# Head tiles staged in two pairs of spare rows, three half projections among the output projections, row stores on the ACT queue, second-product blocks of three pairs

## The chip, the cores and the metric

The kernel runs on one core of a Trainium2 chip, in one launch. The metric is the device time of a run in microseconds (us); lower is better. The engines that matter here are PE (TensorE, the matmuls), DVE (VectorE), ACT (ScalarE), POOL (GpSimd) and SP (SyncE), whose queue issues the DMAs. Every engine works through its own queue in the order in which the program has put the instructions there; an instruction that waits holds up what stands behind it in that queue.

## The reference, cut to what matters

One layer of a diffusion backbone is computed for 1152 tokens (128 context tokens and 1024 latent tokens, nine rows of 128 tokens) of width 1024, in fp32.

```
h = layer_norm(x) * (1 + sc1) + sh1
p = h @ w_in                       # split into DeltaNet (4 heads) and retention (4 heads) inputs and gates
o_a = gated DeltaNet, both directions, RMSNorm, times silu(gate_a)      # 512 columns
o_r = retention, both directions, GroupNorm, times silu(gate_b)         # 512 columns
y = concat(o_a, o_r) @ w_o
x = layer_norm(ALPHA * x + g1 * y, ln1_w, ln1_b)
h = layer_norm(x) * (1 + sc2) + sh2
f = square(relu(h @ w_ff1 + b_ff1)) @ w_ff2 + b_ff2                     # 1024 -> 4096 -> 1024
x = layer_norm(ALPHA * x + g2 * f, ln2_w, ln2_b)
```

Outputs are the new x of both token groups and the final DeltaNet and retention states of the context tokens.

## The kernel before, in words

**Precision.** Every fp32 matmul operand is split into a high part (a cast on ACT, names that end in `h`) and a low part (a subtraction on DVE or POOL, names that end in `l`), and a product is three passes: high by high, low by high, high by low. `split` (L158 cast, L159 subtraction) and `parts_of` (L1369 cast, L1370 subtraction) do this.

**The stages.** The program is a list of small steps in strings (`RET`, `DEL`, `OPS`), which `run` (L267) calls in that order; a number behind `^` lets a step go ahead by that much priority. A scheduler then fixes the order of the instructions on each engine from the program's order and these priorities. The stages run one after the other with overlaps: modulation vectors and first layer norm, retention heads, DeltaNet heads with gate projections, output projection, first feed-forward product, second product, final layer norm.

**The output projection** of a row is in two halves of the 1024 mixed columns. `half_out` (L1003, step R) computes the retention half for row `ORDER[i]`: `heads_in` (L985) loads the gate and the head outputs of the row from DRAM (`GT`, `OT`) into two `wr` tiles, POOL multiplies them (L992), ACT and DVE split the product, and PE runs 24 matmuls of 128x512 (L999). The tag `wr` has two buffers, and the weights' raw tiles use the same tag. The result, scaled and added to ALPHA times the row of x (L1022, L1023), is kept in tiles `hL0` to `hL2`. All nine R steps stand at the end of the DeltaNet stage. In the output stage, `op_load` (L) runs `heads_in` for the DeltaNet half, `op_mm` (M, L1088) runs its 24 matmuls, with a gate multiplication into the tile `gx` (L1097) and an addition into the row (L1098, second half on POOL); `norm1` (A) is the first layer norm with scale (L1105, DVE) and shift (L1106, POOL); `norm2` (B) the second one's statistics (L243, DVE) and normalisation (L253, ACT); `modulate` (C) transposes the row (L1123) and applies the modulation on ACT (L1127).

**The first feed-forward product** is a seven-product scheme (Strassen-like) on pairs of 128-column blocks of `w_ff1`: 16 pairs, each with products named 3, 5, 4, 2, 6, 7, 1 of 24 matmuls of 128x288 (L1194). The token combinations that the products need come from `late_tokens` (T: 3 and 5), `early_tokens` (U: 4 and 2) and `both_tokens` (L1162: 6, 7 and 1; sums at L1143, splits at L1138 and L1139). For the first NB = 3 pairs, products 3 and 5 (`begin_late`, J) run among the output projections and 4 and 2 (`begin_early`) behind them; the two finished quarters of these pairs go to DRAM (`HC`) and come back in `pair` (L1292). A pair ends with squared ReLU (L1201, L1202) and seven operands of the second product stored to DRAM (`HS`): two plain quarters and five sums (L1333), each formed in a stage slot that `next_stage` deals out. There is one slot until pair NB, and three from there on. The last two pairs (14 and 15) store their whole rows to `HR`.

**The second product** takes pairs 0 to 13 in seven blocks of two pairs. A block goes through names 3, 5, 4, 2, 1, 7, 6; for each it loads the stored token operand (`ar`), forms the weight operand from `w_ff2` (L1387 on POOL where it is a sum of two weight blocks), splits both, runs PE (L1404), and DVE adds the result into an accumulator (L1444). The raw weights lie in `w2a` and `w2b`, four buffers each, by `f // 4 % 2`:

```
def w2_raw(f):
    t = sb(fp, [128, 1024], "w2" + "ab"[f // 4 % 2], 4)
    dma(t, w_ff2[128 * f:128 * f + 128, :])
```

In the last block `join` (L1471) merges the accumulators. The four remaining blocks of 128 hidden columns come back from `HR` plain (`last_ff2`), with the residual (L1522, L1523) and the final layer norm behind.

**Queues.** All DMAs, loads and stores, are issued on SP (L84).

## Time and profile before

| | |
|---|---|
| median of 3 runs | 1723.28 us (1723.16 to 1728.45) |
| the profiled execution | 1724.24 us |
| its span | 1722.5 us |
| PE busy | 1528.1 us (89%) |
| DVE busy | 1127.2 us (65%) |
| ACT busy | 740.4 us (43%) |
| POOL busy | 701.2 us (41%) |
| mean granted TensorE clock | 0.945 |

A row of the timeline view gives start and duration in us, engine, line, operation, output and inputs, and in brackets how long the engine stood idle ahead of it and what released it. The table by windows gives for each stretch its length, then the busy time of PE, PE weight loads, DVE, ACT and POOL (with counts of instructions), the granted clock, the DMA share and GB/s. Busy time of one engine covers all of a stretch when it equals the stretch's length. A row by line gives busy time and mean ns of one, then the idle time ahead with what ended it. Line numbers are those of the kernel before.

### The profile page before, as it was taken

How to read it: one execution, taken by the hardware profiler on the slowest of the kernel's cores; microseconds unless marked ns; L12 is line 12 of the kernel's file. 1: busy time of each engine (PE TensorE's matmuls, PEld its weight loads, DVE VectorE, ACT ScalarE, POOL GpSimd, SP SyncE). 2: the span in 40 equal slices, each digit the busy share in tenths (PEclk: the TensorE clock that was granted, in tenths of full speed). 3: DMA queues.
4: the chain of work that ended last, by engine and by line, in shares of the span. 5: the costliest groups of instructions: out<-in, count | busy, mean ns of one | idle time of the engine just before them, and what ended most of it. 6: DMA issues, size and time to landing. Idle time of an engine off the chain costs nothing.

```text
span 1722.5 us, 26166 instructions
## 1 busy us (share of the span) xinstructions
PE 1528.1 (89%) x9657; PEld 1337.6 (78%) x9657; DVE 1127.2 (65%) x1854; ACT 740.4 (43%) x1557; POOL 701.2 (41%) x554
## 2 busy tenths in 40 slices
PE   4899899999999998887676979999968999999584
PEld 2797777898989897775566979999966888888463
DVE  4425245587859683556658445666637788889977
ACT  5522224645546544312566345555535533333132
POOL 2211011211110210115664456665628866667945
PEclk9899999999999998998898989999988999999787
DMA  8333563322230422552223534444437544444032
GB/s 327 100 75 106 167 187 118 81 71 66 54 86 26 96 61 80 186 183 91 72 94 103 183 139 142 141 142 141 139 116 240 177 141 138 139 137 119 25 98 98
DMA packets 188880, 210.23 MB, mean 122 GB/s; under 512 B 32404, under 2 KB 139009, under 8 KB 188625
## 3 DMA queue, kind: packets, MB, share of 16 engines
q1 hardware_dynamic: 188753, 208.57, 38.6%
q8 instruction: 76, 1.25, 0.3%
q14 instruction: 51, 0.42, 0.1%
HBM read 151.18 MB, written 53.14 MB: 119 GB/s over the span
## 4 chain that ended last, share of the span: by engine, by line
PE 48%; POOL 8%; DVE 8%; DMA 5%; ACT 4%; issue 4%; SPq 0%; POOLq 0%; DVEq 0%; ACTq 0%
PE d L1404 17%; PE d L1194 15%; PE mm L192 7%; PE d L999 2%; DMA wr<-OT 1%; DVE wl L159 1%; DMA w<-in_w_ff_dram 1%; POOL mrow L1522 1%; PE c L898 1%; DVE lnst L243 1%; PE c L882 1%; POOL wr L992 1%; PE c L889 1%; PE co L913 1%; POOL hL L1106 1%
## 5 line engine op out<-in xcount | busy, mean ns | idle before, releaser
L159 DVE TENSOR_TENSOR wl<-wr,wh 128x512 fp32r<-128x512 f32 (+1 forms) x160 | 146.3, 916 | 155.8 <-ACT wh L158 151.5
L192 PE MATMUL mm<-hH,wh 128*128 128x384 f32 x672 | 238.9, 356 | 1.8 <-ACT raw L632 1.8
L192 PE MATMUL mm<-hL,wh 128*128 128x384 f32 x672 | 237.5, 353 | 0.0
L192 PE MATMUL mm<-hH,wl 128*128 128x384 f32 x672 | 236.0, 352 | 0.0
L1404 PE MATMUL d<-vh,sh 128*128 128x512 f32 x456 | 183.4, 403 | 37.5 <-ACT sh L1369 17.3
L1194 PE MATMUL d<-q,wh 128*128 128x288 f32 x896 | 197.2, 302 | 17.2 <-ACT wh L158 9.6
L1404 PE MATMUL d<-vh,sl 128*128 128x512 f32 x456 | 183.4, 402 | 10.5 <-DVE sl L1370 10.5
L158 ACT CAST wh<-wr 128x512 fp32r<-128x512 f32 (+1 forms) x160 | 97.5, 612 | 206.4 <-POOL wr L992 60.1
L1404 PE MATMUL d<-vl,sh 128*128 128x512 f32 x456 | 181.8, 400 | 0.0
L1194 PEld LDWEIGHTS d<-q,wh 128*128 128x128 f32 x896 | 151.8, 194 | 18.4 <-ACT wh L158 11.1
L1194 PE MATMUL d<-q,wl 128*128 128x288 f32 x512 | 153.6, 300 | 4.0 <-DVE wl L159 4.0
L1370 DVE TENSOR_TENSOR sl<-ar,sh 128x512 fp32r<-128x512 f32 x106 | 119.4, 1144 | 45.0 <-ACT sh L1369 45.0
L1404 PEld LDWEIGHTS d<-vh,sh 128*128 128x128 f32 x456 | 88.8, 195 | 59.6 <-ACT sh L1369 17.6
L192 PEld LDWEIGHTS mm<-hH,wh 128*128 128x128 f32 x672 | 128.9, 192 | 7.0 <-issue 2.1
L192 PEld LDWEIGHTS mm<-hL,wh 128*128 128x128 f32 x672 | 128.8, 192 | 5.4 <-issue 4.1
L192 PEld LDWEIGHTS mm<-hH,wl 128*128 128x128 f32 x672 | 128.6, 191 | 4.7 <-issue 3.7
L1370 POOL TENSOR_TENSOR vl<-ws,vh 128x512 fp32r<-128x512 f32 x70 | 102.9, 1472 | 66.5 <-ACT vh L1369 66.4
L1369 ACT CAST sh<-ar 128x512 fp32r<-128x512 f32 x106 | 64.2, 621 | 114.6 <-PE d L1404 88.4
L1404 PEld LDWEIGHTS d<-vh,sl 128*128 128x128 f32 x456 | 88.5, 194 | 31.9 <-DVE sl L1370 13.8
L1404 PEld LDWEIGHTS d<-vl,sh 128*128 128x128 f32 x456 | 88.6, 194 | 18.8
L1194 PEld LDWEIGHTS d<-q,wl 128*128 128x128 f32 x512 | 99.2, 194 | 4.7 <-DVE wl L159 4.7
L1194 PE MATMUL d<-hL,wh 128*128 128x288 f32 x384 | 90.8, 299 | 3.4 <-ACT hH L1216 1.8
(376 smaller groups left out, 3679.2 us busy)
## 6 DMA issues: line engine op xcount, KB each, us to landing
ar<-HS SPq DMA_DIRECT2D x98, 256.0 KB
wm<-in_w_mod_dram SPq DMA_DIRECT2D x32, 512.0 KB
w<-in_w_ff_dram SPq DMA_DIRECT2D x32, 512.0 KB
wr<-in_w_in_dram SPq DMA_DIRECT2D x56, 256.0 KB
...
```

The lines of the kernel that those rows point to most:

```text
L158: S.copy(out=pool_hi, in_=src)
L159: V.tensor_tensor(out=pool_lo, in0=src, in1=pool_hi.bitcast(F32), op=ALU.subtract)
L192: T.matmul(p[:, 0:384], x[:, k % 4, :], y[c][:, k, :], start=(k == 0 and a == 0), stop=(k == 7 and a == 2),)
L243: V.bn_stats(out=st[:, j, :], in_=x[:, 512 * j:512 * j + 512])
L882: T.matmul(p[:, 0:128], qk[:, 0, off(n):off(n) + 128], old, start=True, stop=True)
L889: T.matmul(p[:, 0:128], UP[:, m_, 0, :], r, start=True, stop=True)
L898: T.matmul(p[:, 0:128], kt[:, n, :], y2, start=True, stop=True)
L999: T.matmul(p, x[y][k], wo[k0 + k][z][:, js], start=(first and a == k == 0), stop=(last and a == 2 and k == 3))
L1194: T.matmul(p[:, q, :], w[x][:, k, :], hs[y][:, k, CH * q:CH * q + CH], start=(k == 0 and a == 0), stop=(k == 3 and a == 2),)
L1369: S.copy(out=hi, in_=src)
L1370: eng.tensor_tensor(out=lo, in0=src, in1=hi.bitcast(F32), op=ALU.subtract)
L1404: T.matmul(p, x, w, start=(first and i == a == 0), stop=(last and i == n - 1 and a == 2))
```

## The change

1. `heads_in` no longer uses `wr` tiles for gate and heads: they are halves of two of six spare rows of 1024 (`spare[3]` and `spare[4]`, in the tile `hH2`), taken in turn. The spare rows are taken when the first head load is built. The rows of x use three spare rows instead of five.
2. The steps R6, R7 and R8 move from the end of the DeltaNet stage into the output stage, behind M2, A1 and A2, and the steps of that stage stand in another order; there both halves share one PSUM tile.
3. `gx` is a tile of 512 for each half.
4. In `norm2`, rows 1, 3 and 5 get their statistics from two passes on ACT instead of DVE.
5. The token sums of products 6 and 1 move from DVE to POOL.
6. NB goes from 3 to 4, with two more stage tiles: one slot for the early pairs as before, five from pair NB on.
7. The stores of `HC`, `HP`, the plain quarters of `HS`, and `HR` go on the ACT queue.
8. The second product has blocks of 2, 3, 3, 3 and 3 pairs; the first block is built 500 ahead in priority.
9. Of the last operands' four split chains, the second half's subtraction goes to POOL.

```diff
...
-DEL = "... W^1000 n2 t2^150 s3^400 G3^50 n3^400 O^150 R0 t3^50 R1^1000 R2 R3 R4 R5 R6 R7 R8"
-OPS = "L0 M0 L1 L2 L3 M1 A0 L4 M2 B0 A1 M3 C0 L5 B1 A2 M4 C1 L6 B2 A3 M5 C2 L7 T0 B3 A4 M6 C3 L8 B4 A5 M7 C4 T1 B5 A6 M8 C5 B6 A7 J0 C6 B7 A8 J1 C7 B8 J2 U1 C8 U0"
+DEL = "... W^1000 n2 t2^150 s3^400 G3^50 n3^400 O^150 R0 t3^50 R1^1000 R2 R3 R4 R5"
+OPS = "L0 M0 L1 L2 M1 A0 M2 R6 B0 A1 R7 C0 B1 A2 R8 L3 C1 M3 L4 B2 A3 M4 L5 C2 B3 A4 M5 L6 C3 T0 B4 A5 M6 L7 C4 B5 A6 M7 L8 T1 C5 B6 A7 M8 C6 B7 A8 J0 C7 B8 J1 U1 C8 J2 U0 J3"
...
+
+    def act_dma(out, in_):
+        nc.scalar.dma_start(out=out, in_=in_)
...
     wo = {}
     ORDER = (5, 4, 6, 7, 8, 3, 2, 1, 0)
-    parts, spare = [], []
+    parts, spare, turn = [], [], [3, 4]
     def heads_in(k, t):
-        oh, ol, o = w_tiles()
-        g_ = sb(wpool, [128, 4, 128], "wr", 2)
+        oh, ol = sb(wpool, [128, 4, 128], "wh", 4, F32R), sb(wpool, [128, 4, 128], "wl", 4, F32R)
+        if not spare:
+            for n in ("hH1", "hH2"):
+                z = flat(sb(hpool, [128, 8, 384], n, 1))
+                spare.extend(z[:, 1024 * j:1024 * j + 1024] for j in range(3))
+        turn.reverse()
+        g_, o = (spare[turn[0]][:, 512 * j:512 * j + 512].rearrange("p (k t) -> p k t", k=4) for j in range(2))
         m = 4 if k else 3
         for x, src in ((g_, GT), (o, OT)):
             dma(x[:, 0:m], src[128 * k:128 * (k + m), 128 * t:128 * t + 128].rearrange("(k p) t -> p k t", p=128))
...
     def half_out(i):
         x = heads_in(4, ORDER[i])
-        if i == 0:
-            for n in ("hH1", "hH2"):
-                z = flat(sb(hpool, [128, 8, 384], n, 1))
-                spare.extend(z[:, 1024 * j:1024 * j + 1024] for j in range(3))
         if i in (0, 8):
             m = min(ORDER[i], 1)
             dma(spare[5], GD[m:m + 1, :].to_broadcast([128, 1024]))
-        xt = spare[i % 5]
+        xt = spare[i % 3]
         dma(xt, xrow(ORDER[i]))
         if i % 3 == 0:
             parts.append(flat(sb(hpool, [128, 8, 384], f"hL{(2, 0, 1)[i // 3]}", 1)))
         dst = parts[i // 3][:, 1024 * (i % 3):1024 * (i % 3) + 1024]
+        pp = pd() if i > 5 else None
         for j in range(2):
-            p = (pss, pmm)[j]()
             js = slice(512 * j, 512 * j + 512)
+            p = pp[:, js] if i > 5 else (pss, pmm)[j]()
             out_mm(p, x, 4, js, True, True)
             V.tensor_tensor(out=dst[:, js], in0=p, in1=spare[5][:, js], op=ALU.mult)
         V.scalar_tensor_tensor(out=dst, in0=xt, scalar=ALPHA, in1=dst, op0=ALU.mult, op1=ALU.add)
...
     def op_mm(i):
         t = ORDER[i]
         x = oht.pop(i)
-        y = sb(op, [128, 1024], "gx", 2)
         r = parts[i // 3][:, 1024 * (i % 3):1024 * (i % 3) + 1024]
         p = pd()
         for j in range(2):
             js = slice(512 * j, 512 * j + 512)
             out_mm(p[:, js], x, 0, js, True, True)
-            V.tensor_tensor(out=y[:, js], in0=p[:, js], in1=g1[min(t, 1)][:, js], op=ALU.mult)
-            (G if j else V).tensor_tensor(out=r[:, js], in0=r[:, js], in1=y[:, js], op=ALU.add)
+            y = sb(op, [128, 512], "gx", 2)
+            V.tensor_tensor(out=y, in0=p[:, js], in1=g1[min(t, 1)][:, js], op=ALU.mult)
+            (G if j else V).tensor_tensor(out=r[:, js], in0=r[:, js], in1=y, op=ALU.add)
         rt[i] = r
     def norm1(i):
...
     def norm2(i):
         n2[i] = sb(op, [128, 1024], "n2", 2)
         r = rt.pop(i)
-        act_normalise(op, n2[i], r, stats(op, r, 1024, 1e-6))
+        if i in (1, 3, 5):
+            fin["trash"] = n2[i]
+            mv = act_stats(op, r, 1024, 1e-6)
+        else:
+            mv = stats(op, r, 1024, 1e-6)
+        act_normalise(op, n2[i], r, mv)
     def modulate(i):
         t = ORDER[i]
...
     def both_tokens():
         for name, u, v, op_, eng, places in (
-            ("6", "12", "11", ALU.add, V, ((fq, "z0"), (fq, "z1"))), ("7", "21", "22", ALU.add, G, ((ow, "q1"), (ow, "q3"))),
-            ("1", "22", "11", ALU.add, V, ((ow, "q0"), (ow, "q2"))),
+            ("6", "12", "11", ALU.add, G, ((fq, "z0"), (fq, "z1"))), ("7", "21", "22", ALU.add, G, ((ow, "q1"), (ow, "q3"))),
+            ("1", "22", "11", ALU.add, G, ((ow, "q0"), (ow, "q2"))),
         ):
             parts_ = [combine(name, q, fq, "af", 3, u, v, op_, eng) for q in (1, 0)]
             H[name] = [htile(*z) for z in places]
...
     NP, NS = 16, 14
-    HC = [dram.tile([2, 128, TH], F32, name=f"HC{p}") for p in range(3)]
+    HC = [dram.tile([2, 128, TH], F32, name=f"HC{p}") for p in range(4)]
     HS = [dram.tile([7, 128, 512], F32, name=f"HS{p}") for p in range(NS)]
     HP = [dram.tile([128, 2, 128], F32, name=f"HP{p}") for p in range(NS)]
     HR = {f: dram.tile([128, NT], F32, name=f"HR{f}") for f in range(2 * NS, 2 * NP)}
...
         V.tensor_tensor(out=two(c11), in0=two(x), in1=m, op=ALU.add)
         V.tensor_tensor(out=two(c22), in0=two(y), in1=m, op=ALU.add)
-    NB = 3
+    NB = 4
     def slots():
         if not XY:
             z = flat(sb(hpool, [128, 8, 384], "hH0", 1))
-            XY["z"] = [z[:, TH * j:TH * j + TH] for j in range(5)] + [sb(oq, [128, TH], f"xy{j}", 1) for j in range(2)]
-            XY["stage"] = XY["z"][6:]
+            XY["z"] = [z[:, TH * j:TH * j + TH] for j in range(5)] + [sb(oq, [128, TH], f"xy{j}", 1) for j in range(4)]
+            XY["stage"] = XY["z"][8:]
         return XY["z"]
     def hold(p):
...
         c12 = next_stage()
         late_products(x, y, c12, w3, w5)
         squared_relu(c12, 2 * p)
-        dma(HC[p][0], c12)
+        act_dma(HC[p][0], c12)
     def begin_early(p):
         a = w1_raw(p, 1, 1)
...
         c21 = next_stage()
         early_products(x, y, c21, w4, w2)
         squared_relu(c21, 2 * p + 1)
-        dma(HC[p][1], c21)
+        act_dma(HC[p][1], c21)
     w1s = {}
...
         squared_relu(c11, f)
         squared_relu(c22, f + 1)
         if p >= NS:
-            dma(HR[f], af)
-            dma(HR[f + 1], ag)
+            act_dma(HR[f], af)
+            act_dma(HR[f + 1], ag)
             return
         a11, a21, a12, a22 = (z[:, 128 + 512 * j:640 + 512 * j] for z in (af, ag) for j in range(2))
-        dma(HP[p][:, 0, :], af[:, 0:128])
-        dma(HP[p][:, 1, :], ag[:, 0:128])
-        dma(HS[p][2], a11)
-        dma(HS[p][3], a22)
+        act_dma(HP[p][:, 0, :], af[:, 0:128])
+        act_dma(HP[p][:, 1, :], ag[:, 0:128])
+        act_dma(HS[p][2], a11)
+        act_dma(HS[p][3], a22)
         for name, u, v, op_, eng in (
             (4, a11, a12, ALU.add, G), (1, a21, a22, ALU.add, V), (0, a11, a22, ALU.add, G),
             (6, a12, a22, ALU.subtract, V), (5, a21, a11, ALU.subtract, G),
...
             dma(HS[p][name], s_)
     run(OPS, dict(
-        L=op_load, M=op_mm, A=norm1, B=norm2, C=modulate, T=late_tokens, U=early_tokens, J=begin_late,
+        L=op_load, M=op_mm, A=norm1, B=norm2, C=modulate, T=late_tokens, U=early_tokens, J=begin_late, R=half_out,
     ))
     close_op()
     fq, close_fq = pool("fq")
...
         PROMPT = {"3": (1, 0, True, False), "5": (1, 2, False, True), "4": (0, 1, True, False), "2": (0, 2, False, True)}
-        def block(b, after):
+        def block(b, ps, after):
             nonlocal b2
-            ps = (2 * b, 2 * b + 1)
             raws = [[w2_raw(2 * p), w2_raw(2 * p + 1)] for p in ps]
             pp = None
             prompts = None
...
                 if after and name in after:
                     after[name]()
-        for b in range(NS // 2 - 1):
-            block(b, None)
+        BLOCKS = ((0, 1), (2, 3, 4), (5, 6, 7), (8, 9, 10), (11, 12, 13))
+        tc.cur_priority -= 500
+        for b, ps in enumerate(BLOCKS[:-1]):
+            block(b, ps, None)
+            if b == 0:
+                tc.cur_priority += 500
         def join(into, others, engines):
...
         def after7():
             join("4", [("7", ALU.add)], (V, G))
-        block(NS // 2 - 1, {"2": after2, "1": after1, "7": after7})
+        block(len(BLOCKS) - 1, BLOCKS[-1], {"2": after2, "1": after1, "7": after7})
         acc = {0: pacc}
         for z in range(2):
             for j in range(4):
...
             for j in range(2):
                 raw = sb(fp, [128, 512], "ar", 4)
                 dma(raw, HR[f][:, 128 + 512 * j:640 + 512 * j])
-                x.append(parts_of(raw, "s", V))
+                x.append(parts_of(raw, "s", G if j else V))
             t = sb(fp, [128, 3, 128], "pr", 2)
             dma(t[:, 0], HR[f][:, 0:128])
             hi, lo = sb(fp, [128, 3, 128], "ph", 4, F32R), sb(fp, [128, 3, 128], "pl", 4, F32R)
```

The SP queue at the end of the first product, before (`w1` are `w_ff1` loads, `af` and `ag` both print as `af`; what stands in brackets are the semaphores waited for, DMAHW being DMA completions):

```order
L84 DMA w1_12457<-in_w_ff1_dram 128x4x256 [waits DMAHW7_49]
L84 DMA HR28_7849<-af_12220 128x1152 [waits DMAHW0_49,DVE_49,Activation_49]
L84 DMA HR29_7850<-af_12221 128x1152 [waits DMAHW1_49,DVE_49,Activation_49]
L84 DMA HR30_7851<-af_12460 128x1152 [waits DMAHW2_49,DVE_49,Activation_49]
L84 DMA HR31_7852<-af_12461 128x1152 [waits DMAHW3_49,DVE_49,Activation_49]
L84 DMA w2a_12706<-in_w_ff2_dram 128x1024 [waits DMAHW4_49,PE_49]
L84 DMA w2a_12708<-in_w_ff2_dram 128x1024 [waits DMAHW5_49]
```

and with the change:

```order
L84 DMA w1_12434<-in_w_ff1_dram 128x4x256 [waits DMAHW7_49,Activation_49]
L84 DMA w2a_12683<-in_w_ff2_dram 128x1024 [waits DMAHW4_49,PE_49]
L84 DMA w2a_12685<-in_w_ff2_dram 128x1024 [waits DMAHW5_49]
L84 DMA w2a_12687<-in_w_ff2_dram 128x1024 [waits DMAHW6_49]
L84 DMA w2a_12689<-in_w_ff2_dram 128x1024 [waits DMAHW7_49]
```

The four `HR` stores have left the place ahead of the first `w_ff2` loads; on ACT the last two of them now stand between the last squared ReLU and the first cast of the second product.

The SP queue at the first head loads of `half_out`, before (`GT` holds the gates, `OT` the heads' outputs):

```order
L84 DMA wr_7402<-GT_72 128x4x128 [waits DMAHW2_49,DVE_49]
L84 DMA wr_7401<-OT_71 128x4x128 [waits DMAHW3_49,DVE_49]
L84 DMA wr_7472<-GT_72 128x4x128 [waits DMAHW5_49,Pool_49]
L84 DMA wr_7471<-OT_71 128x4x128 [waits DVE_49]
L84 DMA GT_72<-gt_7329 128x384 [waits Activation_49]
L84 DMA wr_7511<-GT_72 128x4x128 [waits DMAHW7_49,Pool_49]
L84 DMA wr_7510<-OT_71 128x4x128 [waits DVE_49]
L84 DMA hH1_7408<-in_x_sample_dram 128x1024 [waits PE_49]
L84 DMA GT_72<-gt_7357 128x384 [waits DMAHW4_49,Activation_49]
```

and with the change:

```order
L84 DMA GT_72<-gt_7357 128x384 [waits Activation_49]
L84 DMA hH2_7402<-GT_72 128x4x128 [waits PE_49]
L84 DMA hH2_7402<-OT_71 128x4x128 [waits DMAHW4_49]
L84 DMA GT_72<-gt_7385 128x384 [waits DMAHW5_49,Activation_49]
L84 DMA hH2_7402<-GT_72 128x4x128 [waits DMAHW6_49]
L84 DMA hH2_7402<-OT_71 128x4x128 [waits DMAHW7_49]
```

Before, three pairs of head loads stand ahead of the last but one store of gates, and none waits for PE; with the change the first pair stands behind it, and its target is a tile that PE reads in the gate projections.

DVE in the middle of the output stage, from one row's gate multiplication (`gx`) to the next row's, before (BN_STATS are the layer norms' statistics, rsqrt steps included):

```order
L1097 TENSOR_TENSOR gx_8111<-d_8112,g1_7862 128x512 [waits PE_49]
L159 TENSOR_TENSOR wl_8337<-wr_8339,wh_8336 128x384 [waits Activation_49]
L243 BN_STATS lnst_8176<-hL2_7412 128x6 [waits Pool_49]
L243 BN_STATS lnst_8176<-hL2_7412 128x6
L243 BN_STATS lnst_8186<-hL0_7557 128x6
L245 BN_AGGR lnmv_8179<-lnst_8176 128x2 [waits DVE_49]
L243 BN_STATS lnst_8186<-hL0_7557 128x6
L246 TENSOR_SCALAR lnmv_8179<-lnmv_8179 128x1 [waits DVE_49]
L247 TENSOR_SCALAR lnmv_8179<-lnmv_8179 128x1
L245 BN_AGGR lnmv_8189<-lnst_8186 128x2 [waits DVE_49]
L1097 TENSOR_TENSOR gx_8199<-d_8200,g1_7862 128x512 [waits PE_49]
```

and with the change, for a row whose predecessor's second statistics are on ACT:

```order
L1102 TENSOR_TENSOR gx_8151<-d_8123,g1_7730 128x512 [waits PE_49]
L162 TENSOR_TENSOR wl_8398<-hH2_7402,wh_8397 128x384 [waits Activation_49,Pool_49]
L246 BN_STATS lnst_8187<-hL0_7549 128x6 [waits Pool_49]
L1102 TENSOR_TENSOR gx_8213<-d_8200,g1_7730 128x512 [waits PE_49]
```

The statistics that wait for POOL's shift of the row before (the rows behind L1105 and L1106) no longer stand between the two `gx` here; for the other rows they still do.

More of the change, by code (lines that the diff above doesn't have):

```diff
@@ L28 @@
 RET = "V2 K0 Q0^150 Z0 V0 S0 O0 V1^400 S1^2500 D^150 N0^150 T0 O1^1000 M1 Q1 N1^2500 T1 K1 Z1^50 M2^1000 M3^50 S2 M0^50 O2^2500 V3^150 N2 S3 T2 O3^1000 N3^1000 T3^50"
-DEL = "P0 i0 v0^1000 P1^50 m0^2500 G1 i1 G5 v1^150 b0 s0 P2 G6 b1^50 n0 t0^6000 m1 i2^150 v2 s1 P3 i3 n1 b2^1000 t1^2500 m2 G7 v3 s2^50 G0^150 G4 b3^2500 G2 m3 W^1000 n2 t2^150 s3^400 G3^50 n3^400 O^150 R0 t3^50 R1^1000 R2 R3 R4 R5 R6 R7 R8"
-OPS = "L0 M0 L1 L2 L3 M1 A0 L4 M2 B0 A1 M3 C0 L5 B1 A2 M4 C1 L6 B2 A3 M5 C2 L7 T0 B3 A4 M6 C3 L8 B4 A5 M7 C4 T1 B5 A6 M8 C5 B6 A7 J0 C6 B7 A8 J1 C7 B8 J2 U1 C8 U0"
+DEL = "P0 i0 v0^1000 P1^50 m0^2500 G1 i1 G5 v1^150 b0 s0 P2 G6 b1^50 n0 t0^6000 m1 i2^150 v2 s1 P3 i3 n1 b2^1000 t1^2500 m2 G7 v3 s2^50 G0^150 G4 b3^2500 G2 m3 W^1000 n2 t2^150 s3^400 G3^50 n3^400 O^150 R0 t3^50 R1^1000 R2 R3 R4 R5"
+OPS = "L0 M0 L1 L2 M1 A0 M2 R6 B0 A1 R7 C0 B1 A2 R8 L3 C1 M3 L4 B2 A3 M4 L5 C2 B3 A4 M5 L6 C3 T0 B4 A5 M6 L7 C4 B5 A6 M7 L8 T1 C5 B6 A7 M8 C6 B7 A8 J0 C7 B8 J1 U1 C8 J2 U0 J3"
 NEG = -1.0e30
```

## The prediction

> **What bounds the kernel now.** I read the page first (busy shares; slices), then a table by windows that cuts the span at the stages, then the timeline where that table shows idle time.
>
> ```profile
> PE 1528.1 (89%) x9657; PEld 1337.6 (78%) x9657; DVE 1127.2 (65%) x1854; ACT 740.4 (43%) x1557; POOL 701.2 (41%) x554
> PE   4899899999999998887676979999968999999584
> PEclk9899999999999998998898989999988999999787
> ...
> 716.00:774.00 58.00, 51.84 (x225) 40.99 (x223) 31.29 (x41) 9.23 (x16) 10.47 (x8) 0.98 0.65 212
> 774.00:914.00 140.00, 93.75 (x434) 76.61 (x434) 87.58 (x153) 72.89 (x134) 83.68 (x72) 0.84 0.25 82
> 914.00:960.00 46.00, 40.09 (x268) 38.95 (x268) 37.43 (x39) 21.63 (x31) 18.11 (x12) 0.91 0.42 132
> 960.00:1040.00 80.00, 69.02 (x485) 67.92 (x484) 39.22 (x53) 33.89 (x56) 41.16 (x31) 0.94 0.46 160
> 1040.00:1260.00 220.00, 220.00 (x1661) 220.00 (x1660) 142.68 (x158) 111.02 (x179) 131.01 (x89) 1.00 0.40 135
> 1260.00:1300.00 40.00, 20.71 (x142) 19.16 (x141) 11.75 (x14) 11.28 (x19) 12.18 (x10) 0.76 0.43 159
> 1300.00:1600.00 300.00, 300.00 (x1314) 248.16 (x1315) 249.04 (x234) 128.62 (x227) 216.52 (x152) 0.99 0.48 152
> 1600.00:1640.00 40.00, 18.68 (x52) 12.12 (x50) 39.67 (x23) 4.53 (x8) 38.24 (x17) 0.65 0.08 22
> ```
>
> PE bounds the kernel: it is busy without a break from 1040 to 1260 and from 1300 to 1600, at a clock of 0.99 to 1.00. What an edit saves on another engine in those stretches is worth nothing. The idle time lies in four places: the output projection (140.00 − 93.75 = 46.3 us, clock 0.84), the two stretches behind it (5.9 and 11.0), the passage between the feed-forward products (19.3, clock 0.76) and the end of the second product (21.3, clock 0.65). The change leaves PE's matmuls as many as they were, so it can win only idle time and clock in these places, or bring in new waits.
>
> **The change part by part.** The sum is made against the profiled execution's 1724.24 us, 1.0 above the median of 1723.28.
>
> *A. Stores to HR off the SP queue.* SP's timeline, the chain of waits, and PE's timeline at the passage:
>
> ```profile
> 1258.66 23.18 SPq L84 DMA_DIRECT2D HR<-af  x4
> 1281.93 3.03 SPq L84 DMA_DIRECT2D w2a<-in_w_ff_dram  x4
> ...
> 1280.82 0.68 ACT af L1202
> 1282.70 6.87 DMA w2a<-in_w_ff_dram
> 1289.74 1.27 POOL ws L1387
> 1291.03 0.63 ACT vh L1369
> 1294.76 0.62 ACT sh L1369
> 1295.43 0.79 PE L1404 MATMUL d<-vh,sh 128*128 128x512 f32 x1 [17.35 <-ACT sh L1369]
> ```
>
> The four stores sit on SP from 1258.66 on and wait for the last squared ReLU (ended 1281.50). Behind them stand the first `w_ff2` loads, and behind those the load of 6.87, POOL, two casts, and PE after 17.35 us of idling. With the change the loads go out about 1259 and everything up to the casts is ready while products still run. What is late next is ACT: ReLU to 1281.5, two store issues (0.4 each, as on SP), two casts of `vh` at 0.63 and one of `sh` at 0.62, so PE starts at about 1284.3. That is 1295.43 − 1284.3 = 11.1, and about 1 more since the `sl` chains, behind `sh`, also come earlier. **−12**, bounds −13 and −9 (an ACT store held 2 to 3 us by an earlier DMA on its lane).
>
> The Trainium skill speaks against this edit (DMA: Bandwidth & Descriptors, section Issuing engines are not separate DMA queues): DMAs from several engines end on the same 16 DMA engines, and issuing from more saves only issue time. By it the edit would be worth some 1 us and the sum would come out at 1703. The trace does not agree for this place: the 23.18 us on SP is no transfer but a store that waits in order ahead of loads that need not.
>
> *B. Half projections and head loads.* POOL, SP and PE at the half projections:
>
> ```profile
> 715.66 0.33 PE L192 MATMUL mm<-hH,wl 128*128 128x384 f32 x1
> 715.84 0.39 PE L999 MATMUL s<-q,wh 128*128 128x512 f32 x1
> ...
> 743.75 0.38 SPq L84 DMA_DIRECT2D wr<-OT  x1
> 747.05 1.30 POOL L992 TENSOR_TENSOR wr<-wr 128x512 f32<-128x512 f32 x1 [4.71 <-DMA wr<-OT]
> ...
> 774.09 0.79 PE L999 MATMUL d<-q,wh 128*128 128x512 f32 x1 [4.86 <-ACT wh L158]
> 774.68 0.80 PE L999 MATMUL d<-q,wl 128*128 128x512 f32 x1
> 779.34 0.40 PE L999 MATMUL d<-q,wh 128*128 128x512 f32 x1
> ```
>
> Before, the first half projection starts right behind the last gate matmul, since three head loads were done by then. Now the first load's target is in `hH2`, which that gate product reads, so it goes out only at about 716: 0.4 for the first issue, 3.3 from the second issue to POOL (743.75 to 747.05), 1.3 on POOL, 0.6 for the cast: 5.6 us of idle PE. After the 4.86 us wait at 774.09, 12 matmuls took 5.25 us to 779.34, against 12 × 0.228 = 2.7 at full clock (300.00 over 1314 matmuls of this shape): 2.5 more. **New stall +8**, bounds 0 (the tile comes free earlier) and +10. The nine half projections took 715.84 to 769.23, 5.9 each; three of them leave the line: **−17.8**, if their PE work fits into the output stage's idle 46. The wait of 4.86 ahead of the first output projection and its slow clock go, as its heads can now load two ahead: **−7.4**.
>
> *C. The ring of the output projections.*
>
> ```profile
> PE d L999 <- DVE gx L1097: 27.0, 8, 5.5
> ...
> 839.28 0.64 DVE L1097 TENSOR_TENSOR gx<-d,g 128x512 f32<-128x512 f32 x1
> 845.62 2.21 POOL L1098 TENSOR_TENSOR hL<-hL,gx 128x512 f32<-128x512 f32 x1 [2.53 <-DVE gx L1097]
> 847.80 2.78 POOL L1106 TENSOR_TENSOR hL<-hL,l1b 128x1024 f32<-128x1024 f32 x1
> 850.61 1.88 DVE L243 BATCH_NORM_STATS2 lnst<-hL 128x6 f32<-128x512 f32 x3 [2.23 <-POOL hL L1106]
> 853.32 0.64 DVE L1097 TENSOR_TENSOR gx<-d,g 128x512 f32<-128x512 f32 x1
> ```
>
> PE's second half waits for `gx` of the first (27.0 us in eight waits). `gx` stands on DVE behind statistics that wait for POOL's shift of the row before; a row takes 853.32 − 839.28 = 14.0 us. For rows 1, 3 and 5 these statistics are now on ACT, and `gx` waits only for POOL's 2.21 (ended 847.83) and half the statistics: about 849 instead of 853.3, so 3 × 4 = 12 less. Against that the three half projections bring DVE a split (0.7), two multiplications (0.64 each) and a row pass (1.3 by its neighbours): 3.3 × 3 = 10 more in the same ring, if none of it fits into DVE's free 52 us. **−2**, bounds −15 and +12.
>
> *D. The fourth early pair.*
>
> ```profile
> DVE xy L1333 <- DMA HS<-xy: 15.8, 5, 5.9
> L84 SPq DMA_DIRECT2D HS<-xy x18: 319/320/448, 963.1 to 1028.7; - x18
> L1143 DVE TENSOR_TENSOR af<-q,q x4: 1341/1350/1699, 916.8 to 938.4; 128x1152 f32<-128x1152 f32 x4
> L1143 POOL TENSOR_TENSOR af<-q,q x2: 2677/3202/3726, 907.5 to 924.1; 128x1152 f32<-128x1152 f32 x2
> ```
>
> A product takes 24 × 0.1325 = 3.2 us (220.00 over 1661). Products 3 and 5 of pair 3 move from full PE into idle time: −6.3. Its sums now pass the single slot: 18 issues from 963.1 to 1028.7 are 3.86 us each, five sums 19.3 us a pair, against 3 × 3.2 = 9.5 us of PE work left in such a pair: +10 (0 to +16). **+3.7.** The five slots afterwards serve a stretch where PE has no gap: 0.
>
> *E. Sums for products 6 and 1 on POOL:* four leave DVE at 1.35 each (5.4), busy 37.4 of 46.0 there; on POOL they take 2.7 to 3.7. **−4**, bounds −5 and 0.
>
> *F. Blocks of three pairs* take 14 accumulator additions a block less for two blocks, 28 × 1.2 = 34 us of DVE; PE covers it, so 0. The price is the raw weights: four buffers of each kind hold four pairs, a block and the next need six. Two pairs of each later block can load only once POOL has formed the last sums of the block before. Unhidden that is the passage of A again, up to 17.35 each at three boundaries. Names 1, 7, 6 of three pairs are 3 × 36 matmuls, 24.6 us of cover, against 6.87 + 1.27 + 0.63 and POOL's second operation of 1.5: **+3** in all, bounds 0 and +52.
>
> *G. The end of the second product.* DVE's and POOL's rows by line there, and DVE's over 1300 to 1600:
>
> ```profile
> L1522 POOL TENSOR_TENSOR mrow<-mrow,w2a 128x1024 f32<-128x1024 f32 x8 | 21.0, 2647 | 1.8 <-DVE mrow L1471 1.8
> L1370 DVE TENSOR_TENSOR sl<-ar,sh 128x512 fp32r<-128x512 f32 x7 | 16.3, 2364 | 0.0
> L1444 DVE TENSOR_TENSOR mrow<-mrow,d 128x1024 f32<-128x1024 f32 x46 | 55.8, 1213 | 10.6 <-PE d L1404 10.6
> L1370 DVE TENSOR_TENSOR sl<-ar,sh 128x512 fp32r<-128x512 f32 x97 | 100.3, 1052 | 29.2 <-ACT sh L1369 29.1
> ```
>
> DVE (39.67) and POOL (38.24) are both full from 1600 to 1640, and a split takes 2364 ns instead of 1052. The last three names grow from 5.4 to 8.1 us each, 8 us more cover for the joins; moving four splits from one full engine to the other gives little. **−4**, bounds −8 and +3.
>
> The Trainium skill (SBUF — State Buffer, section SBUF: two separate sides) has it that a DVE operation with two SBUF inputs and a POOL operation exclude each other for a whole instruction. The doubled split agrees. By it alone E and G would be worth nothing and the sum would be 1700.
>
> **Sum:** −12 + 8 − 17.8 − 7.4 − 2 + 3.7 − 4 + 3 − 4 = −32.5; 1724.24 − 32.5 = 1691.7, and 1.0 less as the median stands: **1691 us**.
>
> **The rivals.**
>
> *The output ring lengthens* and takes back what leaves the line: C at +12, D at +10, E and G at 0. −12 + 8 − 17.8 − 7.4 + 12 + 10 + 3 = −4: 1719. For it: each moved step adds work to DVE, on which the ring turns, and POOL is already 60% busy there. Against: the idle 46 us of PE and DVE's 52. Chance 0.17.
>
> *The ring opens further*, since all rows gain from two head loads ahead and `gx` tiles of a half: five more rows at 2 to 4 us, some −18: 1673. For it: the ring is made of waits, not of work. Against: rows 0, 2, 4 keep the statistics on DVE. Chance 0.15.
>
> *Slower: the blocks' boundaries show.* F at +52, less the other terms' −35.5: 1740. It decides from 35.5 / 3 = 11.8 us a boundary on. For it: SP's queue holds the operand loads behind a `w_ff2` load that waits for POOL, which is 216.52 of 300.00 busy. Against: 24.6 us of cover. Chance 0.09.
>
> *The ACT queue is held by its new stores,* so the gain doesn't come: a store that waits up to 3 us on its lane holds the casts behind it, in twelve pairs some 36 us, and the sum is +3: 1726. Against: ACT is 111.02 of 220.00 busy in the full stretch. Chance 0.04.
>
> **How the numbers follow.** The forecast has 0.55, with a range of its own of 1677 to 1704. To hold 8 in 10, the range takes in the opened ring and most of the lengthened one: 1667 to 1718. About 0.3% (5 us) is what a measurement of this kernel can tell from no change. Faster: 0.55 + 0.15 + 0.12 = 0.82; within: 0.05 of the lengthened ring and 0.02 of the held queue = 0.07; slower: 0.11.
>
> **What would show it.** A: PE's wait ahead of its first L1404 matmul falls from 17.4 to about 6, and no HR store on SP. B: a wait of about 5.6 us for ACT's cast in front of the first half projection; no 4.86 ahead of the first output projection. C: rows about 10 and 14 us apart in turn. D: waits for the slot's stores grow by half. F: no PE wait above 3 us between blocks. The forecast is wrong if PE idles between blocks, or if the stretch from the last gate to the first full pair is not shorter by 15 us or more.

## The result, and the profile after

The changed kernel takes 1739.88 us (median of six runs, 1735.12 to 1744.83) against 1724.43 (six runs, 1723.16 to 1728.45): a ratio of 1.0083, 95% interval 1.0061 to 1.0104. It is **15 us slower**; 1691, within 1667 to 1718, was forecast. The profiled execution of the changed kernel is the slowest of its six (1744.83, span 1743.0), so its trace shows some 5 us more than the median does.

From the page of the changed kernel:

```profile
PE 1547.4 (89%) x9657; PEld 1354.3 (78%) x9657; DVE 1117.1 (64%) x1804; ACT 749.7 (43%) x1572; POOL 720.6 (41%) x562
PE   5899999899999998797667978999997999999575
PEclk9899999999999996898877998999998999999787
```

PE has the same 9657 matmuls, 19 us more busy (busy time at a lower granted clock counts as busy), and the same weak places: digits 16 to 25 (before 16 to 24) hold the output projections and what follows, digit 31 the passage between the products, the last three the end. The table by windows of the changed kernel, cut at its own stages:

```profile
722.00:732.00 10.00, 0.65 (x3) 0.38 (x2) 0.40 (x1) 1.54 (x3) 2.52 (x2) 0.71 0.94 327
732.00:769.00 37.00, 37.00 (x155) 29.95 (x155) 28.05 (x36) 7.90 (x16) 10.89 (x9) 0.94 0.77 240
769.00:918.00 149.00, 107.41 (x457) 86.07 (x456) 91.47 (x146) 71.48 (x132) 73.23 (x68) 0.83 0.23 76
918.00:960.00 42.00, 30.20 (x157) 28.27 (x157) 30.20 (x18) 22.26 (x34) 29.18 (x12) 0.74 0.31 98
960.00:1027.00 67.00, 63.66 (x468) 62.78 (x467) 38.68 (x49) 25.95 (x41) 30.22 (x23) 0.99 0.50 167
1027.00:1063.00 36.00, 21.79 (x144) 21.18 (x144) 13.33 (x19) 12.64 (x20) 15.44 (x12) 0.81 0.45 149
1063.00:1310.00 247.00, 243.69 (x1823) 243.47 (x1824) 167.72 (x171) 122.42 (x195) 138.29 (x95) 0.99 0.40 142
1310.00:1319.00 9.00, 0.74 (x4) 0.45 (x3) 1.78 (x3) 4.73 (x8) 4.04 (x4) 0.69 0.36 143
```

Two idle stretches are new: 10 us in front of the first half projection, and 14 us between 1027 and 1063, in the middle of the pairs, where before PE was nearly full. The output projections (769 to 918) still idle for 41.6 us although they now contain three half projections, and 11.8 us are lost from 918 to 960. Only the passage at 1310 is shorter.

To put the difference in its place I took the first and last starts of PE's lines. Rows by source line, first those of before, then those of the changed kernel (output projection, transposes, first feed-forward product, second product):

```profile
L1123 PE MATMUL d<-ident,n x72: 270/273/421, 809.2 to 904.2; 128*128 128x128 f32 x72
L1194 PE MATMUL d<-q,wl x512: 292/296/445, 915.3 to 1277.8; 128*128 128x288 f32 x171
L1404 PE MATMUL d<-vh,sh x456: 387/389/796, 1295.4 to 1708.1; 128*128 128x512 f32 x152
```

```profile
L1007 PE MATMUL d<-q,wh x156: 389/397/796, 768.6 to 894.5; 128*128 128x512 f32 x156
L1133 PE MATMUL d<-ident,n x72: 270/273/477, 799.0 to 917.3; 128*128 128x128 f32 x72
L1204 PE MATMUL d<-q,wl x512: 292/296/609, 945.5 to 1310.1; 128*128 128x288 f32 x171
L1414 PE MATMUL d<-vh,sh x456: 388/389/794, 1318.7 to 1728.0; 128*128 128x512 f32 x152
```

The lengths of the stages between such starts, in us (with two variants that are described below):

| stage | before | changed | difference | changed, with three early pairs, three slots, sums and statistics on DVE (g1) | fastest (g4) |
|---|---|---|---|---|---|
| start to last gate matmul | 715.7 | 721.9 | +6.2 | 717.9 | 712.6 |
| to first half projection | 0.1 | 9.7 | +9.6 | 9.7 | 0.2 |
| to first output projection | 58.3 | 37.0 | −21.3 | 36.4 | 42.6 |
| to last transposes | 130.1 | 148.7 | +18.6 | 134.5 | 139.7 |
| to last matmul of the first product | 373.6 | 392.8 | +19.2 | 367.4 | 359.8 |
| to first matmul of the second product | 17.6 | 8.6 | −9.0 | 8.6 | 8.6 |
| to last matmul of the second product | 413.2 | 410.1 | −3.1 | 412.0 | 414.1 |
| to the end | 13.9 | 14.2 | +0.3 | 14.2 | 13.7 |

The first row is no effect of the change: the last gate matmul starts between 712.6 and 721.9 in the fourteen profiles of this study, and the change does not touch the work up to there but for its last head loads.

The two stages on either side of the last transposes do not hold the same work. Before, 144 matmuls of the first product start ahead of the last transposes; with the new order of the steps only 96 do. The other 48, 6.4 us at the 0.134 us that one takes from 1063 to 1310 (243.69 over 1823), stand behind them. So 6.4 of the 19.2 us are work that has moved into that stage, and the output stage is 18.6 us longer although it has that much less of it.

### The profile page after: what moved, and what is told of

Read it like the earlier page. It is cut to its first block, busy times and chain, and to the rows that moved or that the text cites. A ratio compares the mean times of both kernels' runs of the same rounds, so it can differ in the third digit from the quotient of the medians.

```text
span 1743.0 us, 26118 instructions
## 1 busy us (share of the span) xinstructions
PE 1547.4 (89%) x9657; PEld 1354.3 (78%) x9657; DVE 1117.1 (64%) x1804; ACT 749.7 (43%) x1572; POOL 720.6 (41%) x562
## 4 chain that ended last, share of the span: by engine, by line
PE 55%; DVE 7%; POOL 6%; DMA 4%; issue 3%; ACT 2%; SPq 0%; DVEq 0%; POOLq 0%; ACTq 0%
PE d L1204 17%; PE d L1414 17%; PE mm L195 9%; PE d L1007 2%; DMA HS<-xy 1%; PE c L901 1%; PE s L1007 1%; PE c L892 1%; PE mm L1007 1%; PE c L885 1%; PE co L916 1%; PE co L915 1%; POOL af L1153 1%; PE s L696 1%; PE c L821 1%
## 5 line engine op out<-in xcount | busy, mean ns | idle before, releaser
L162 DVE TENSOR_TENSOR wl<-wr,wh 128x512 fp32r<-128x512 f32 x144 | 143.4, 1002 | 122.8 <-ACT wh L161 122.3
L1204 PE MATMUL d<-q,wh 128*128 128x288 f32 x896 | 199.0, 304 | 21.3 <-DVE af L1246 14.3
L161 ACT CAST wh<-wr 128x512 fp32r<-128x512 f32 x144 | 88.7, 620 | 127.6 <-PE mm L195 45.2
L1380 DVE TENSOR_TENSOR sl<-ar,sh 128x512 fp32r<-128x512 f32 x102 | 111.0, 1104 | 45.2 <-ACT sh L1379 45.0
L1414 PEld LDWEIGHTS d<-vl,sh 128*128 128x128 f32 x456 | 88.2, 193 | 18.6
L158 POOL TENSOR_TENSOR ms<-ms,ex 128x9 f32<-128x9 f32 (+3 forms) x10 | 16.8, 1682 | 182.2 <-DVE ms L941 106.2
```

What stands on the lines that cost most here:

```text
L161: S.copy(out=pool_hi, in_=src)
L162: V.tensor_tensor(out=pool_lo, in0=src, in1=pool_hi.bitcast(F32), op=ALU.subtract)
L1204: T.matmul(p[:, q, :], w[x][:, k, :], hs[y][:, k, CH * q:CH * q + CH], start=(k == 0 and a == 0), stop=(k == 3 and a == 2),)
L1380: eng.tensor_tensor(out=lo, in0=src, in1=hi.bitcast(F32), op=ALU.subtract)
L1414: T.matmul(p, x, w, start=(first and i == a == 0), stop=(last and i == n - 1 and a == 2))
```

## The experiments

The loss stands in three stages. Two theories were put against each other first. **Slot:** the fourth early pair queues at the single stage slot and costs more than its products save. **Ring:** the output projections lose what the shorter line ahead of them wins. What PE waits for in the new idle stretch of the changed kernel, first its PE rows, then SP's, then the chain of waits:

```profile
1028.47 0.50 PE L1204 MATMUL d<-q,wh 128*128 128x288 f32 x2 [3.00 <-DVE af L1246]
...
1049.55 0.82 PE L1204 MATMUL d<-q,wh 128*128 128x288 f32 x2 [11.30 <-DVE af L1246]
```

```profile
1017.84 10.04 SPq L84 DMA_DIRECT2D HS<-xy  x4
...
1040.37 8.60 SPq L84 DMA_DIRECT2D HS<-xy  x3
```

```profile
1029.69 1.30 POOL xy L1343
1031.02 4.68 DMA HS<-xy
...
1035.85 1.30 POOL xy L1343
...
1037.58 3.89 DMA w<-in_w_ff_dram
...
1045.81 2.00 DMA HS<-xy
...
1047.92 0.70 DVE xy L1343
```

PE waits 11.30 us for a PSUM result to be read by DVE (L1246). That read stands on DVE behind a sum (L1343), the sum waits for the slot, and the slot is free only when the store before has landed (2.0 to 4.7 us each). SP, whose queue holds these stores, holds the next pair's weights behind them: their load of 3.89 us goes out at 1037.58, right behind a store, and POOL's next sum stands behind it.

**e1: three early pairs.** The changed kernel with

```diff
-    NB = 4
+    NB = 3
-... C8 J2 U0 J3"
+... C8 J2 U0"
```

> The changed kernel with three early pairs instead of four (its one stage slot for them, and five afterwards, kept). Theory S (the single slot): the fourth pair's five sums queue up behind each other at the slot and hold DVE and PE; without it the PE idle time after the first full pairs goes, about 15 to 20 us less than the changed kernel: 1720 to 1725. Theory R (the output ring): the loss is in the output projections, and the fourth pair is worth its 6 us of products; then this comes out at 1740 to 1746.

Measured: 1727.84 us (ratio to before 1.0021, interval 1.0005 to 1.0037), 12 us less than the changed kernel; the stage up to the last matmul of the first product falls from 392.8 to 381.6. The slot theory holds, though with 12 us rather than 15 to 20. What remains (381.6 is still 8 more than before) is for the most part the 48 matmuls that come later with the new order (6.4 us).

**e2: three early pairs, three slots.** As e1 with

```diff
-            XY["stage"] = XY["z"][8:]
+            XY["stage"] = XY["z"][6:]
```

> As the run with three early pairs, but these have three stage slots (the rows that the fourth pair no longer needs) instead of one. Theory S: waits for a stored sum go nearly to nothing before pair 3; another 5 to 10 us less than with one slot: 1713 to 1718. Rival: with three pairs the slot is hidden by PE work, no difference to one slot (within 3 us).

Measured: 1718.76 us (0.9968, 0.9955 to 0.9981), 9 us less than e1; the stage falls to 371.5. Waits for the slot, from the lists of waits of the changed kernel and of e2:

```profile
DVE xy L1343 <- DMA HS<-xy: 19.3, 8, 3.7
POOL xy L1343 <- DMA HS<-xy: 13.3, 5, 3.8
```

```profile
DVE xy L1343 <- DMA HS<-xy: 6.4, 2, 3.4
POOL xy L1343 <- DMA HS<-xy: 2.5, 2, 2.3
```

32.6 us of waiting become 8.9; in e1 they are 18.5 (17.3 on DVE, 1.2 on POOL), so the fourth pair and the missing slots each have a share. The one slot was a cost already with three pairs, in the kernel before too (15.8 us of such waits on DVE and 13.7 on POOL, 29.5 in all). Four pairs with more than one slot were not tried, so that the fourth pair's 12 us are the slot's alone is read from these waits and not shown by a run.

**e3: the three half projections back.** The changed kernel with

```diff
-DEL = "... R4 R5"
+DEL = "... R4 R5 R6 R7 R8"
-OPS = "... M2 R6 B0 A1 R7 C0 B1 A2 R8 L3 ..."
+OPS = "... M2 B0 A1 C0 B1 A2 L3 ..."
```

and each half in a PSUM tile of its own, as before.

> The changed kernel with the half projections 6, 7 and 8 back at the end of the DeltaNet stage. By the prediction's term B they were worth 17.8 us of line time less 10 us in the ring: this should be about 8 to 16 us slower than the changed kernel, 1748 to 1756. Theory R: the ring is lengthened by as much as the line is shortened, so within 4 us of the changed kernel, 1736 to 1744.

Measured: 1745.01 us (1.0126, 1.0089 to 1.0163), 5 us more than the changed kernel, between the two theories; the intervals of the two overlap. In the profile, gate to first output projection grows by 16.6 us and the output stage shrinks by 9.8 (148.7 to 138.9). The move pays, but more than half is given back in the ring. And the ring without any half projection, 138.9, is longer than before (130.1): something else lengthens it (f3).

**e4: the kernel before with the HR stores on ACT.**

```diff
-            dma(HR[f], af)
-            dma(HR[f + 1], ag)
+            nc.scalar.dma_start(out=HR[f], in_=af)
+            nc.scalar.dma_start(out=HR[f + 1], in_=ag)
```

> The kernel before, only the four HR stores issued on ACT's queue. By the prediction's term A: 12 us less than before, about 1712, PE idle ahead of its first matmul of the second product from 17.4 to about 6 us. Rival: the first matmul comes earlier but the time is given back at the end of the second product, where DVE and POOL are full: within 3 us of before.

Measured: 1716.94 us (0.9957, 0.9938 to 0.9976), 7.8 us less than before. SP's row, ACT's and PE's at the passage:

```profile
1264.98 1.76 SPq L84 DMA_DIRECT2D w2a<-in_w_ff_dram  x4
...
1284.87 0.62 ACT L1369 CAST vh<-ws 128x512 fp32r<-128x512 f32 x1 [0.45 <-ACT af L1202]
1288.08 0.62 ACT L1369 CAST vh<-ws 128x512 fp32r<-128x512 f32 x1 [2.59 <-POOL ws L1387]
1289.28 0.80 PE L1404 MATMUL d<-vh,sh 128*128 128x512 f32 x1 [8.27 <-ACT sh L1369]
```

The loads go out 17 us earlier (1264.98 instead of 1281.93), and PE idles 8.27 us instead of 17.35. The second cast waits 2.59 for POOL, whose two operations for the second weight sum come after the first cast; that is the part of the forecast 12 which did not come. Nothing is given back later: the second product takes 413.2 us in both profiles.

The remaining loss in the first product and the longer ring were looked for next, on e2 as the base.

**f1: token sums back on DVE.** As e2 with

```diff
-("6", "12", "11", ALU.add, G, ...  ("1", "22", "11", ALU.add, G, ...
+("6", "12", "11", ALU.add, V, ...  ("1", "22", "11", ALU.add, V, ...
```

> The run with three early pairs and three slots, with the token sums of products 6 and 1 back on DVE. The prediction's term E (these sums on POOL win 4 us): 1723. Rival P (POOL is late: six sums of about 3 us in a row stand ahead of the first full pair): 5 to 10 us less, 1709 to 1714, and the stretch from the last transposes to the last product of the first feed-forward product shorter by that.

Measured: 1712.83 us (0.9931, 0.9907 to 0.9954), 5.9 us less than e2. POOL's rows in e2, then the 47 us behind the last transposes in e2 and in f1:

```profile
929.38 13.58 POOL L1153 TENSOR_TENSOR af<-q,q 128x1152 f32<-128x1152 f32 x4
942.92 1.27 POOL L1282 TENSOR_TENSOR wr<-wr 128x512 f32<-128x512 f32 x1
```

```profile
912.60:960.00 47.40, 35.52 (x200) 33.76 (x199) 38.92 (x27) 25.24 (x38) 31.06 (x14) 0.79 0.30 93
```

```profile
909.30:957.00 47.70, 38.78 (x228) 37.73 (x227) 37.60 (x33) 26.58 (x40) 20.09 (x11) 0.79 0.34 111
```

Four sums in a row hold POOL for 13.58 us, and the weight sum (L1282) that `begin_early`'s products need stands behind them. With the sums on DVE PE is busy 3.3 us more there, and DVE isn't fuller (37.60 against 38.92). The rival P has the right sign and place, but its size is open: 3.3 of the 5.9 us are seen in this stretch, and the stage up to the last matmul of the first product, which P had 5 to 10 us shorter, is 1.8 shorter here (371.5 to 369.7) and 5.4 shorter in g1 against f3 (372.8 to 367.4).

**f2: blocks of two pairs.** As e2 with

```diff
-BLOCKS = ((0, 1), (2, 3, 4), (5, 6, 7), (8, 9, 10), (11, 12, 13))
+BLOCKS = ((0, 1), (2, 3), (4, 5), (6, 7), (8, 9), (10, 11), (12, 13))
```

> The run with three early pairs and three slots, with the second product in seven blocks of two pairs again (first block still ahead in priority). The prediction's terms F and G (+3 and -4) nearly cancel: within 3 us, 1716 to 1722. Rival W (the blocks' weight loads show): 5 us or more less, with PE waits at block boundaries gone. Rival J (three pairs cover the joins): 4 to 8 us more, with a longer end of the second product.

Measured: 1722.61 us (0.9988, 0.9967 to 1.0010), 3.9 us more than e2, with overlapping intervals of the ratio. The second product grows from 409.3 to 416.8 in the profiles. No weight load shows at a boundary of the larger blocks: from 1319 to 1616 PE of the changed kernel is busy 295.06 of 297.00. Whether the blocks are worth 0 or 4 us stays open (see g2).

**f3: statistics back on DVE.** As e2 with

```diff
-        if i in (1, 3, 5):
+        if i in ():
```

> The run with three early pairs and three slots, with all second statistics on DVE. The prediction's term C (the ACT statistics open the ring by 12 us): 5 to 12 us slower, 1724 to 1731. Rival L (the two passes on ACT make the chain to the transposes longer, on which PE then waits): 4 to 9 us faster, 1710 to 1715, with PE's waits of transposes for the normalised row down from 18 to about 10 us.

Measured: 1707.09 us (0.9886, 0.9842 to 0.9930), 11.7 us *less* than e2. Rows by line in the output stage, of e2, then of f3:

```profile
L1102 DVE TENSOR_TENSOR gx<-d,g 128x512 f32<-128x512 f32 x18 | 12.3, 682 | 16.0 <-PE d L1007 16.0
L1133 PE MATMUL d<-ident,n 128*128 128x128 f32 x72 | 12.3, 323 | 18.3 <-ACT n L256 18.3
```

```profile
L1102 DVE TENSOR_TENSOR gx<-d,g 128x512 f32<-128x512 f32 x18 | 12.1, 672 | 3.2 <-PE d L1007 3.2
L1133 PE MATMUL d<-ident,n 128*128 128x128 f32 x72 | 10.6, 296 | 8.8 <-ACT n L256 8.8
```

With the ACT statistics DVE did get to `gx` sooner: it then waited 16.0 us for PE. But PE was waiting elsewhere: 18.3 us for ACT's normalised row in front of the transposes. In f3 that wait is 8.8, and gate to last transposes falls from 194.3 to 181.1. An engine was relieved and the wait moved to the one that took the work. How such a row comes to be late can be read from the longest of these waits in e2 (rows of ACT, DVE, POOL, ACT and PE):

```profile
840.19 1.15 ACT L1148 CAST hH<-d 128x1152 fp32r<-128x1152 f32 x1 [5.01 <-POOL d L1153]
841.25 1.05 ACT L263 ACTIVATE hL<-hL 128x1024 f32<-128x1024 f32 x1
...
847.83 0.14 DVE L266 TENSOR_SCALAR lnmv<-lnmv 128x1 f32<-128x1 f32 x1
847.98 2.34 POOL L1111 TENSOR_TENSOR hL<-hL,l1b 128x1024 f32<-128x1024 f32 x1 [1.16 <-DVE lnmv L266]
850.28 0.55 POOL L158 TENSOR_TENSOR lnmv<-lnmv,ex 128x1 f32<-128x1 f32 x1
...
851.13 1.24 ACT L256 ACTIVATE n<-hL,lnmv 128x1024 f32<-128x1024 f32 x1 [4.73 <-POOL lnmv L255]
852.42 1.97 PE L1133 MATMUL d<-ident,n 128*128 128x128 f32 x8 [8.05 <-ACT n L256]
```

The first pass (L263) stands behind a cast that waited 5.01 us for POOL. The second pass and its read-out end at 846.40. What is left of the statistics are small steps on other engines, and they wait in order too: the one on DVE (L266) starts at 847.83, behind another row's scale, and the one on POOL (L158) at 850.28, behind another row's shift of 2.34 us. So the row is normalised from 851.13 on, 4.7 us after both passes were done.

**f4: the kernel before with HR stores on ACT and more slots.**

```diff
-            ... + [sb(oq, [128, TH], f"xy{j}", 1) for j in range(2)]
+            ... + [sb(oq, [128, TH], f"xy{j}", 1) for j in range(4)]
```

with e4's edit, and `gx` in halves as in the change.

> The kernel before with the four HR stores on ACT, gx tiles of a half, and two more stage tiles, so that early pairs have three slots and later ones five. If the two gains add (8 us of the stores as measured, 9 us of the slots as between one and three slots at three pairs): 1706 to 1710. Rival: the slot costs less where the sums of products 6 and 1 are on DVE; then 1712 to 1717.

Measured: 1700.08 us (0.9854, 0.9819 to 0.9889), 24.5 us less than before and 16.9 less than e4, more than both expectations. The stage up to the last matmul of the first product falls from 373.6 to 360.0. The waits for the slot:

```profile
DVE xy L1333 <- DMA HS<-xy: 6.8, 3, 3.4
POOL xy L1333 <- DMA HS<-xy: 3.5, 2, 1.9
```

29.5 us of waits became 10.3 on these two engines; ACT waited once for such a store, 6.4 us. The halves of `gx` were not tried alone, but they act in the output stage, which is no shorter (128.7 in e4, 129.5 here). The slots are the largest lever that was found.

**g1: sums and statistics back on DVE.** As e2 with the edits of f1 and f3.

> The changed kernel with three early pairs, three slots, and both the token sums and the second statistics back on DVE. If the parts add, 1707 less 6: 1701. Rival: both free the same wait of PE ahead of the first full pair, then it stays at 1705 to 1708.

Measured: 1702.43 us (0.9869, 0.9831 to 0.9907), 4.7 us less than f3: the two nearly add up (16.3 of 11.7 + 5.9).

**g2: f4 with blocks of three pairs,** the changed kernel's `BLOCKS` and its priority of the first block.

> The kernel before with HR stores on ACT, three and five stage slots, and the second product in blocks of three pairs (first block ahead in priority). If the blocks are worth 4 us here as in the changed kernel: 1696. Rival: within 2 us of the run without the blocks, 1698 to 1702.

Measured: 1701.05 us (0.9862, 0.9823 to 0.9901), 1 us from f4. The blocks of three can't be told from blocks of two here.

**g3: head loads back in the wr tiles.** As g1 with

```diff
-        g_, o = (spare[turn[0]][:, 512 * j:512 * j + 512]...)
+        oh, ol, o = w_tiles()
+        g_ = sb(wpool, [128, 4, 128], "wr", 2)
```

> As the run with sums and statistics on DVE, with the head loads back in the two wr tiles. Theory H (the head rows in the tile of the gates' input cost a stall of about 9.6 us in front of the first half projection and save 5 to 7 us at the first output projection): 2 to 5 us faster, the first half projection within 1 us of the last gate matmul. Rival (prediction's term B, the two rows ahead carry the three moved half projections): with one load at a time these wait in the output stage, and the time is 5 us or more longer.

Measured: 1698.20 us (0.9843, 0.9810 to 0.9877), 4.2 us less than g1 with ranges that do not overlap (1695.58 to 1700.88, and 1701.12 to 1704.58). First rows of the half projections in the changed kernel (SP, POOL, ACT, PE):

```profile
722.30 0.38 SPq L84 DMA_DIRECT2D hH<-GT  x1
722.73 0.51 SPq L84 DMA_DIRECT2D hH<-OT  x1
...
727.67 1.26 POOL L1000 TENSOR_TENSOR hH<-hH 128x512 f32<-128x512 f32 x1 [10.14 <-DMA hH<-OT]
729.66 1.26 POOL L1000 TENSOR_TENSOR hH<-hH 128x512 f32<-128x512 f32 x1 [0.73 <-DMA hH<-OT]
...
730.95 1.14 ACT L161 CAST wh<-hH 128x512 fp32r<-128x512 f32 x2 [8.10 <-POOL hH L1000]
731.62 0.79 PE L1007 MATMUL s<-q,wh 128*128 128x512 f32 x1 [9.35 <-ACT wh L161]
```

The stall is as forecast in kind and 9.35 us long. In g3 it is gone (0.2), and the first output projection waits 7.0 us for its cast again, as the theory had it. In the single pair of profiles the stretch from the gates to the end of the first product is equal (548.0 and 548.3), so where the 4 us of the medians lie is not shown: of the 5.6 us between the two profiles, 4.0 lie ahead of the last gate matmul, and 2.0 in the second product.

**g4: g2 with half projections 6, 7 and 8 among the output projections,** head loads in `wr` tiles:

```diff
-DEL = "... R4 R5 R6 R7 R8"
+DEL = "... R4 R5"
-OPS = "L0 M0 L1 L2 L3 M1 A0 L4 M2 B0 A1 M3 C0 L5 B1 A2 M4 C1 ..."
+OPS = "L0 M0 L1 L2 M1 A0 M2 R6 B0 A1 R7 C0 B1 A2 R8 L3 L4 M3 L5 M4 C1 ..."
```

> As the kernel before with HR stores on ACT, slots and blocks of three, with half projections 6, 7 and 8 among the first output projections, head loads in wr tiles. If their 17 us of PE work fits into the output stage's idle time as predicted: 10 to 16 us faster, 1681 to 1687. As in the changed kernel (5 us): 1691. Rival: the one-at-a-time head loads now serve both kinds of projection in the same stretch, and nothing is won: 1695 or more.

Measured: **1692.82 us** (0.9810, 0.9779 to 0.9840), 8.2 us less than g2 and 32 less than before: the fastest of all. The gain lies between the two expectations (10 to 16, and 5): about half of the moved 17 us fits into the output stage's idle time. Against g3, g4 is 5.4 us faster, with ranges that do not overlap. The two differ only in the order of the steps in the output stage, in the stores of `HC`, `HP` and the plain quarters of `HS` (on SP in g4), and in the last operands' split. In the profiles the difference lies ahead of the second product (from the last gate matmul to the end of the first product 542.3 against 548.3), and g4 has 144 matmuls of the first product ahead of the last transposes, g3 96. That speaks for the order of the steps; it was not tried alone.

## Why the prediction was wrong, point by point

| term | forecast | measured | from |
|---|---|---|---|
| A, HR stores off SP | −12 | −7.8 | e4 against before |
| B, three half projections moved, with the +10 that C has for them in the ring | −7.8 | −5.1 and −8.2 | e3 against the changed kernel; g4 against g2 |
| B, head rows: stall, and wait at the first output projection | +8 −7.4 | +4.2 | g1 against g3 |
| C, statistics on ACT (the −12 in its −2) | −12 | +11.7 | e2 against f3 |
| D, fourth early pair | +3.7 | +12.0 | changed kernel against e1 |
| E, token sums on POOL | −4 | +4.7 and +5.9 | f3 against g1; e2 against f1 |
| F and G, blocks of three, the end | −1 | −3.9 and +1 | e2 against f2; g2 against f4 (both the blocks alone) |

The forecast column adds up to −32.5. With −5.1, +5.9 and −3.9 the measured column adds up to +17.0; the whole change measures +15.5. That is near, within what medians of 4 to 10 runs can tell, but it is no proof that the list is complete: the terms were measured from different bases (C, E and B's head rows with three early pairs and three slots), B's head rows have no place in the profiles (g3), and the order of the steps, the other stores on ACT and the last operands' split were not undone alone (g4). Forecast and measurement lie 48 us apart; C makes up half of that (23.7), E and D most of the rest (9.9 and 8.3).

*The bound* was read rightly: only idle time and clock can be won, and nearly all that was won or lost lies in the four places and the two new gaps. Of the 34 us that the blocks take off DVE at most 4 are seen in a time (e2 against f2). The sign that was set for a wrong forecast came: the stretch from the last gate matmul to the last transposes, which stand ahead of the first full pair, is no shorter but 6.9 us longer (188.5 to 195.4).

*A* was right in mechanism. PE's wait fell by 9.1 us (17.35 to 8.27), the median by 7.8. The size failed at "two casts of `vh`": the second one waits 2.59 us for POOL, which I had put as done while products still ran. What the Trainium skill says (DMA: Bandwidth & Descriptors, section Issuing engines are not separate DMA queues), that more issuing engines save only issue time, is not what this place shows: the gain of 7.8 us is waiting in order that has gone.

*B's stall* was right (9.35 for 5.6). The load took from 722.73 to 727.67, 4.9 for 3.3, with the DMA engines at 0.94 and 327 GB/s; and the cast started only when POOL had also ended the second row's product, 730.92. The wait ahead of the first output projection is gone in the changed kernel, as forecast, and back in g3 (7.0). The moved half projections came out nearly as forecast: 17.8 off the line and 10 back in the ring, and the profiles show 16.6 and 9.8 (e3).

*C* is the step that failed worst, in sign. I had followed DVE alone: `gx` no longer waits for POOL's shift. It did come free (16.0 us of waiting for PE). But the statistics didn't vanish: two passes of 1.05 and 1.14 us stood in order on ACT behind a cast that waits for POOL, and their small steps on DVE and POOL behind another row's scale and shift. That made the row's chain to the next transposes longer, and PE waited there 18.3 us instead of 8.8. I costed the work that was moved on the engine it left and at nothing on the engine it went to.

*D* was right in mechanism (the slot), and its size was the error: 10 for the queue, less 6.3 for the products, when it is 12 net. If the products saved their 6.3, the queue cost about 18, beyond my upper bound of 16. The sign for it, waits for the slot's stores up by half, came against e1 (18.5 to 32.6 us) but not against the kernel before (29.5). What I left out is what stands behind a waiting sum: the PSUM read on DVE (11.30 us of PE's waiting) and, on SP, the next pair's weights. I also passed by what was plain in the same row: 29.5 us of waits for one slot in the kernel before, where more slots win 17 us (f4).

*E* failed in sign for the same reason as C: POOL's side was priced as durations, not by what stands behind them. A weight sum for the products that PE needed next waited behind 13.58 us of token sums. The rule of the Trainium skill that was set beside it (SBUF — State Buffer, section SBUF: two separate sides) would have made E worth nothing; the loss of 5 us is more than that, and by the rows of e2 it is a queue in order.

*The rivals.* "The output ring lengthens" had the right place, and the right sign for C and D (1719); its reason, more work on DVE, is not what the rows of e2 show, where PE waits for ACT's normalised row. "The blocks' boundaries show", the slower rival, fell: no such wait is seen. That its 1740 is the measured time is chance. "The ACT queue is held by its stores" is seen only in small: between 960 and 1320 of the changed kernel the list of ACT's waits has 7.3 us for its stores to land (3.8 for `HS<-af`, 2.6 for `HP<-af`, 0.9 for `HC<-xy`), where the rival had 36. What that costs was not tried alone.
